# Seven-product FFN stage: transfers in GpSimd's queue, weight sums earlier, two products ahead of the down projection

## The chip, the cores and the metric

One of the eight cores of one Trainium2 chip runs the kernel. The metric is device time in microseconds of one execution, the median of several; lower is better. Everything is float32 in and out.

## The reference

The reference is a two-layer backbone over 512 latent tokens and 256 context tokens (768 rows of 1024), cut here to the parts that the change touches:

```python
mod = silu(c) @ w_mod          # six vectors of 1024 a layer, for latent (c) and context (c_ctx)
h = rms_norm(x, g) * (1 + scale) + shift
x = x + gate1 * (mix(h) @ w_out)             # mixing sub-layer: gMLP, attention, mLSTM
h = rms_norm(x, g) * (1 + scale2) + shift2
x = x + gate2 * swiglu(h)                     # FFN sub-layer

def swiglu(h, w_gate, w_up, w_down):
    return (jax.nn.silu(h @ w_gate) * (h @ w_up)) @ w_down     # D_FF = 2816
```

The context rows go through the same weights. The second layer's modulation needs only the first two of its six vectors for the context.

## The kernel before, in words

Activations lie transposed, 128 features by tokens, latent 512 and context 256 columns. A float32 product is made of three matmuls in the chip's reduced type: every operand is split into a high part (hi, an ACT activation) and the rest (lo, a DVE subtraction), and hi by hi, hi by lo and lo by hi are summed in PSUM. So each weight tile that arrives by DMA (wraw, 128 x 1024, 512 KB) is split into whi and wlo before its matmuls: by `wload` (L130 for the load, L133 and L134 for the split) for ordinary products, by `split_w` (L113, L114) in the seven-product stage. Matmuls into `dps` are ordinary ones (`dense`, L157).

Each engine has its own queue of instructions, in an order that a scheduler fixes when the kernel is built: it walks the instructions as they are written and places them by due times, so the order in the code and the order in the queue differ, but neither changes at run time. Buffers of a pool are shared in turn: an instruction that needs a buffer waits for the last user of what was in it. The pools that matter are `wraw` (4 buffers; loads of w_seven, of w_dn, and of w_mod, named wmod, all use it), whi/wlo of the stage (3), PSUM in `mm` (3) and `mx` (4), and `za`, seven buffers, four of which hold operands during the stage, so that three are left for xs.

Layer 0's FFN is the stage in question, `ffn_seven`. The gate and up products of one pair of 128-wide column blocks are each computed as one 2 x 2 block product by seven half-size products instead of eight, a scheme of Strassen's kind. A **unit** is one of the 22 such products (11 pairs, gate and up). It loads two weight tiles a and b, and forms sums of their quarters on DVE: `sums` makes s1 and s2 and rewrites b, L1243 to L1245; `w4` makes another one, L1255. Its products P1 and P2 (weights of `w1`, tile a), P6 and P5 (`w2`, from s2 and s1), P7 and P4 (`w3`, tile b), and P3 (`w4`) are 12 matmuls of 128 x 384 each, into PSUM banks X, Y and Z. `stage1` is P1 and P2, `stage2` is sums, w2, P6, P5, w3 and P7, `stage3` is w4, P4 and P3. Program order interleaves two units: the stage2 of one, the stage1 of the next, the stage3 of the first. The products of TensorE are pinned in that order. `snap` copies a bank out, and `put` adds, applies Silu or the product of gate and up, and splits the result into gh and gl (L113, L114, L1293).

After the first pair, and then after every two pairs, comes a **down**: the part of w_dn that belongs to the pairs just made is multiplied with gh and gl and added to the residual. The pieces are `FF0_PIECES`: one with nf = 2 (96 matmuls of 512 or 256 columns, in eight steps k), four with nf = 4 (192 matmuls), and a last one that runs into the next layer's norm. One w_dn tile serves two of the eight steps k. The residual x does not fit beside the operands: it lies in DRAM (xd), and for each k a buffer xs is loaded (L1434), the product is added with the gate by `resid` (two DVE steps, L1106), and xs is stored (L1437). All transfers of the stage stand in the queue of SyncE (SPq).

The downs are also where the second layer's modulation vectors are worked out. `mod_steps` yields items, and `feed` takes some of them after each k: an item loads one 128 x 1024 tile of w_mod (L213) and multiplies it with the broadcast condition on DVE, summing along the row (L216), once for each of the two streams (latent and context), or once only for vectors 2 to 5 of layer 1. With two streams the first step's output goes to a second wraw buffer, called junk. Vectors 1 to 5 of layer 1, forty items, are fed in the stage: four in the first down, nine in each of the next four. Vector 0 of layer 1 and vector 5 of layer 0 are fed in layer 0's w_out (sixteen items, thirty-two DVE steps), one or two a k (`fill_rate`).

## Time and profile before

| | us |
|---|---|
| median of 3 runs | 1750.72 (1750.66 to 1758.18) |
| the profiled execution | 1757.62 |
| its span | 1755.6 |
| mean granted TensorE clock | 0.976 |
| layer 0's w_out | about 405 to 477 |
| seven-product stage with its downs | about 477 to 1052 |
| layer 1's mixing and w_out | up to about 1380 |

The page of the profile lists engine busy times, waits by releaser ("PE dps L157 <- ACT whi L133" is the time in which TensorE stood ahead of a matmul into dps and what it waited for last was ScalarE's whi) and groups of instructions by line. PE is TensorE's matmuls and PEld its weight loads, which run ahead of the matmuls and overlap them. DVE is VectorE, ACT ScalarE, POOL GpSimd, SP SyncE, and SPq the DMA issues in SyncE's queue. A row of a table by stretches has the stretch, its length, the busy time and number of instructions of PE, PEld, DVE, ACT and POOL, the granted TensorE clock, the share of time in which the DMA engines were busy, and GB/s. A row of waits has the total, the number and the longest. Matmul ends are modelled.

### The profile page before, as it was taken

To read this page: it belongs to the slowest core of one execution; us is meant where nothing else is said; L and a number is where in the kernel's file an instruction comes from. 1 tells how busy PE (TensorE), PEld (TensorE's weight loads), DVE (VectorE), ACT (ScalarE), POOL (GpSimd) and SP (SyncE) were. 2 spreads that over 40 slices of the span, in tenths; PEclk is the share of its full clock that TensorE was granted. 3 is DMA by queue.
4 is the path that set the end of the run, shared out by engine and by line. 5 is a ranking of instruction groups with operands and counts; after the bars stand their busy time and mean duration, and the time that the engine had idled before them with its cause. 6 is when DMAs were issued, how large, how long until landed. Compare 5 with 4: busy or idle time off the path is not lost.

```text
span 1755.6 us, 26472 instructions
## 1 busy us (share of the span) xinstructions
PE 1632.7 (93%) x10520; PEld 1422.0 (81%) x10520; DVE 1116.1 (64%) x1987; ACT 697.7 (40%) x1277; POOL 167.7 (10%) x157
## 2 busy tenths in 40 slices
PE   7998989988888989989999999989999999999998
PEld 5876777776777969889898988867879988888888
DVE  5598788779786676757567557585585633333335
ACT  5445344642552414234241445534454522222225
POOL 0001122252100000000000030012043100000000
PEclk9998999999998999999999999999999999999999
DMA  8742323245426264562828252211213322222222
GB/s 304 253 154 61 109 77 94 68 134 171 168 75 240 72 227 145 166 206 97 275 73 278 93 178 87 94 57 38 73 61 118 111 96 97 96 96 96 96 79 84
DMA packets 71403, 223.85 MB, mean 128 GB/s; under 512 B 8432, under 2 KB 10096, under 8 KB 71152
## 3 DMA queue, kind: packets, MB, share of 16 engines
q1 hardware_dynamic: 71280, 222.17, 38.3%
q8 instruction: 82, 1.34, 0.3%
q14 instruction: 41, 0.34, 0.1%
HBM read 195.92 MB, written 26.21 MB: 127 GB/s over the span
## 4 chain that ended last, share of the span: by engine, by line
PE 62%; DVE 19%; DMA 8%; ACT 4%; issue 4%; POOL 2%; SPq 0%; DVEq 0%; ACTq 0%; POOLq 0%
PE dps L157 35%; PE X L1264 8%; DMA wmod<-in_w_mod 4%; PE wps L406 4%; PE Z L1264 3%; PE vps L652 3%; PE Y L1264 2%; DMA wraw<-in_w_dn 2%; DVE wlo L134 2%; DVE wmod L216 2%; DVE junk L216 2%; PE bops L546 1%; DMA xd<-xs 1%; PE ptps L588 1%; DVE wlo L114 1%
## 5 line engine op out<-in xcount | busy, mean ns | idle before, releaser
L133 ACT ACTIVATE whi<-wraw 128x1024 fp32r<-128x1024 f32 (+3 forms) x182 | 183.3, 1008 | 471.5 <-PE dps L157 229.5
L134 DVE TENSOR_TENSOR wlo<-wraw,whi 128x1024 fp32r<-128x1024 f32 (+3 forms) x182 | 215.1, 1183 | 140.4 <-ACT whi L133 135.7
L157 PE MATMUL dps<-gh,whi 128*128 128x512 f32 (+1 forms) x576 | 176.7, 348 | 22.2 <-ACT whi L133 15.6
L157 PE MATMUL dps<-gl,whi 128*128 128x512 f32 (+1 forms) x576 | 175.8, 345 | 0.2 <-DVE gl L114 0.2
L157 PE MATMUL dps<-gh,wlo 128*128 128x512 f32 (+1 forms) x576 | 173.8, 344 | 0.2 <-DVE wlo L134 0.2
L157 PE MATMUL dps<-lh,whi 128*128 128x512 f32 x336 | 137.0, 410 | 4.2 <-ACT whi L133 3.4
L157 PE MATMUL dps<-lh,wlo 128*128 128x512 f32 x336 | 136.4, 407 | 2.0 <-DVE wlo L134 2.0
L157 PE MATMUL dps<-ll,whi 128*128 128x512 f32 x336 | 136.8, 408 | 1.5 <-DVE ll L114 1.4
L157 PEld LDWEIGHTS dps<-gh,whi 128*128 128x128 f32 x576 | 100.2, 191 | 39.2 <-ACT whi L133 17.2
L157 PE MATMUL dps<-h2lh,whi 128*128 128x512 f32 (+1 forms) x336 | 128.0, 384 | 0.0
L157 PE MATMUL dps<-h2ll,whi 128*128 128x512 f32 (+1 forms) x336 | 128.0, 384 | 0.0
L157 PE MATMUL dps<-h2lh,wlo 128*128 128x512 f32 (+1 forms) x336 | 127.9, 384 | 0.0
L216 DVE SCALAR_TENSOR_TENSOR wmod<-wmod,c_all 128x1024 f32<-128x1024 f32 x80 | 101.3, 1266 | 22.4 <-DMA wmod<-in_w_mod 21.7
L157 PEld LDWEIGHTS dps<-gl,whi 128*128 128x128 f32 x576 | 100.6, 192 | 14.4 <-DVE gl L114 0.7
L157 PEld LDWEIGHTS dps<-gh,wlo 128*128 128x128 f32 x576 | 99.7, 190 | 13.8 <-DVE wlo L134 0.5
L1106 DVE SCALAR_TENSOR_TENSOR x<-dps,modT,x 128x256 f32<-128x256 f32 (+1 forms) x80 | 46.9, 589 | 94.8 <-PE dps L157 94.2
L114 DVE TENSOR_TENSOR wlo<-wraw,whi 128x1024 fp32r<-128x1024 f32 (+1 forms) x66 | 67.9, 1043 | 35.7 <-ACT whi L113 35.6
L157 PE MATMUL dps<-ch,whi 128*128 128x256 f32 x256 | 76.4, 298 | 14.2 <-DVE bv L525 7.5
L113 ACT ACTIVATE whi<-wraw 128x1024 fp32r<-128x1024 f32 (+1 forms) x66 | 59.4, 913 | 62.7 <-PE Z L1264 19.0
L1264 PE MATMUL X<-ol,whi 128*128 128x384 f32 x242 | 81.8, 338 | 2.6 <-DVE ol L114 2.6
L1264 PE MATMUL X<-oh,whi 128*128 128x384 f32 x242 | 81.7, 338 | 1.3 <-ACT gate L1283 0.9
L1264 PE MATMUL X<-oh,wlo 128*128 128x384 f32 x242 | 81.5, 337 | 1.0 <-DVE wlo L114 1.0
(382 smaller groups left out, 3891.7 us busy)
## 6 DMA issues: line engine op xcount, KB each, us to landing
wmod<-in_w_mod SPq DMA_DIRECT2D x80, 512.0 KB, 3.8
wraw<-in_w_seven SPq DMA_DIRECT2D x44, 512.0 KB, 3.7
wraw<-in_win_blk SPq DMA_DIRECT2D x34, 512.0 KB, 3.6
xs<-xd SPq DMA_DIRECT2D x40, 384.0 KB, 5.0
xd<-xs SPq DMA_DIRECT2D x40, 384.0 KB, 4.4
wraw<-in_w_out SPq DMA_DIRECT2D x23, 512.0 KB, 3.3
wraw<-in_w_dn SPq DMA_DIRECT2D x22, 512.0 KB, 4.1
wraw<-in_w_up SPq DMA_DIRECT2D x21, 512.0 KB, 3.3
```

The lines of the kernel that those rows point to most:

```text
L113: ac.activation(out=hi, in_=src, func=AF.Copy)
L114: ve.tensor_tensor(out=lo, in0=src, in1=hi.bitcast(F32), op=ALU.subtract)
L133: ac.activation(out=hi[:, 0:n], in_=raw[:, 0:n], func=AF.Copy)
L134: ve.tensor_tensor(out=lo[:, 0:n], in0=raw[:, 0:n], in1=hi[:, 0:n].bitcast(F32), op=ALU.subtract)
L157: m = te.matmul(out=ps[:, 0:T], lhsT=wt[:, c], rhs=(flo if wh else fhi)(k), start=(k == 0 and wi == 0), stop=(k == nk - 1 and wi == 2),)
L216: ve.scalar_tensor_tensor(out=wraw.tile([128, D], F32, tag="w", name="junk") if t < nt - 1 else raw, in0=raw, scalar=1.0, in1=c_all[:, t, ...
L406: m = te.matmul(out=ps[:, 0:T], lhsT=wt[:, cs_], rhs=(flo if wh else fhi)(k), start=(k == 0 and wi == 0), stop=(k == KD - 1 and wi == 2))
L546: m = te.matmul(*args, **kw)
L588: te.transpose(out=tps[:, i * 128:(i + 1) * 128], in_=pt[:, i * 128:(i + 1) * 128], identity=ident)
L652: te.matmul(out=vps[i][:, 0:408], lhsT=tokslice(nm, k, i), rhs=wt[:, cs], start=(k == 0 and wi == 0), stop=(k == KD - 1 and wi == 2))
L1106: ve.scalar_tensor_tensor(out=xs, in0=ps, scalar=modT[:, row * 8 + k, g[3]:g[3] + 1], in1=xs, op0=ALU.mult, op1=ALU.add)
L1264: m = te.matmul(out=ps[:, 0:HN], lhsT=wt[:, c], rhs=O[op, j][wh], start=(start and j == 0 and wi == 0), stop=(j == 3 and wi == 2), skip_gr ...
```

## The change

It has five parts.

1. The loads and stores of the residual in the stage (xs, xd, and the first store and the last load of x) and the modulation loads of the stage are issued by GpSimd (`gp`) in place of SyncE (`sp`). SyncE keeps w_seven and w_dn.
2. An item of modulation in the stage is one stream: one load, one DVE step, no junk buffer. Vectors 0 and 1 of layer 1 are so loaded twice, and the stage has 56 items: vectors 0 to 4 of layer 1. They are fed eight in the first down, and twelve in each of the next four.
3. Vector 0 of layer 1 thus leaves layer 0's w_out, which keeps eight items (vector 5 of layer 0, sixteen DVE steps); vector 5 of layer 1 goes to layer 1's w_out, eight items of one step.
4. The next unit's `sums` and `w2` are written ahead of the stage3 of the current unit.
5. P6 and P5 (`stage2a`) of the unit that follows a down are written ahead of the down, and the down's first matmul is pinned behind them.

The queues at the fourth down (w_dn0_3, the one from 826 us in the profile of before). SyncE before, where in_w_dn0_3 is w_dn, wmod a modulation load and the xd and xs rows are residual transfers:

```order
L130 DMA wraw_7687<-in_w_dn0_3 128x1024
L213 DMA wmod_7721<-in_w_mod 128x1024
L213 DMA wmod_7724<-in_w_mod 128x1024
L213 DMA wmod_7759<-in_w_mod 128x1024
L130 DMA wraw_7765<-in_w_dn0_3 128x1024
L213 DMA wmod_7799<-in_w_mod 128x1024
L213 DMA wmod_7833<-in_w_mod 128x1024
L1437 DMA xd_106<-xs_7685 128x768
L130 DMA wraw_7839<-in_w_dn0_3 128x1024
```

GpSimd now, at the same place:

```order
L1452 DMA xs_7778<-xd_106 128x768
L220 DMA wmod_7738<-in_w_mod 128x1024
L220 DMA wmod_7772<-in_w_mod 128x1024
L220 DMA wmod_7775<-in_w_mod 128x1024
L220 DMA wmod_7815<-in_w_mod 128x1024
L1454 DMA xd_106<-xs_7701 128x768
L220 DMA wmod_7849<-in_w_mod 128x1024
L220 DMA wmod_7852<-in_w_mod 128x1024
L1454 DMA xd_106<-xs_7741 128x768
L1452 DMA xs_7818<-xd_106 128x768
```

The modulation loads and the residual's transfers have left SyncE's queue, where they stood between the w_dn loads, and stand together in GpSimd's; in SyncE's the four w_dn loads of this down now follow one another. All of them still take their buffers from the same four of wraw, two of which the next unit's a and b hold during a down. Of the two others, one takes w_dn and modulation loads in turn now (wraw_7703, wmod_7772, wraw_7780, wmod_7849 and so on), the other modulation loads alone.

VectorE ahead of a unit's P6, before. Tiles a and b of this unit are wraw_5654 and wraw_5655; lines L1243 to L1245 are its sums, the two rows into wlo_5735 its splits for P6 and P5, and the first row, from wraw_5517, is the split for P3 of the unit before it; the rows into gate and sn are `put`:

```order
L114 TENSOR_TENSOR wlo_5692<-wraw_5517,whi_5691 128x512
L1289 TENSOR_TENSOR sn_5632<-sn_5632,X_5525 128x384
L1293 TENSOR_TENSOR gate_5497<-gate_5497,sn_5632 128x384
L114 TENSOR_TENSOR gl_5591<-gate_5497,gh_5589 128x384
L1289 TENSOR_TENSOR gate_5726<-sn_5676,Y_5663 128x384
L1243 TENSOR_TENSOR s1_5729<-wraw_5655 128x512
L1244 TENSOR_TENSOR s2_5730<-s1_5729,wraw_5654 128x512
L1245 TENSOR_TENSOR wraw_5655<-wraw_5654,wraw_5655 128x512
L1293 TENSOR_TENSOR gate_5570<-gate_5570,X_5525 128x384
L114 TENSOR_TENSOR wlo_5735<-s2_5730,whi_5734 128x512
L114 TENSOR_TENSOR wlo_5735<-s1_5729,whi_5734 128x512
```

And now, at a unit of the same kind with tiles wraw_5750 and wraw_5751, where wlo_5792 is the split for P6 and P5, and wlo_5799 that for P3 of the unit before it:

```order
L1250 TENSOR_TENSOR s1_5786<-wraw_5751 128x512
L1251 TENSOR_TENSOR s2_5787<-s1_5786,wraw_5750 128x512
L1252 TENSOR_TENSOR wraw_5751<-wraw_5750,wraw_5751 128x512
L114 TENSOR_TENSOR wlo_5792<-s1_5786,whi_5791 128x512
L1296 TENSOR_TENSOR gate_5730<-gate_5730,X_5625 128x384
L114 TENSOR_TENSOR wlo_5792<-s2_5787,whi_5791 128x512
L1262 TENSOR_TENSOR wraw_5750<-wraw_5750,s2_5787 128x512
L1296 TENSOR_TENSOR sn_5772<-sn_5772,Y_5759 128x384
L114 TENSOR_TENSOR wlo_5799<-wraw_5617,whi_5798 128x512
L1300 TENSOR_TENSOR gate_5700<-gate_5700,sn_5772 128x384
```

The three sums and the two splits stood behind the split for P3 of the unit before and four steps of its outputs; they now stand ahead of that split. On TensorE P6 and P5, 24 matmuls into X and Z that stood behind each down's dps rows, stand ahead of them.

The diff (line numbers of the changed kernel are 7 to 18 higher in the stage):

```diff
@@ -114,7 +114,7 @@
         ve.tensor_tensor(out=lo, in0=src, in1=hi.bitcast(F32), op=ALU.subtract)
 
     fill = []
-    last_pe = [None]
+    last_pe, pin_d = [None], [None]
     fill_rate = [FILL_MIX]
 
     chain = [None]
@@ -158,6 +158,9 @@
                         out=ps[:, 0:T], lhsT=wt[:, c], rhs=(flo if wh else fhi)(k),
                         start=(k == 0 and wi == 0), stop=(k == nk - 1 and wi == 2),
                     )
+                    if pin_d[0] is not None:
+                        after(m, pin_d[0])
+                        pin_d[0] = None
                     if i == 1:
                         if share not in (None, True) and k == 0 and wi == 0:
                             after(m, share[1])
@@ -204,19 +207,23 @@
 
     c_all = const.tile([128, 2, D], F32, name="c_all")
 
-    def mod_steps(l, vs):
+    def mod_steps(l, vs, single=False):
         modT, sm = mods[l], smalls[l]
-        items = [(v, i) for v in vs for i in range(KD)]
-
-        def step(v, i):
+        nts = {v: 1 if l == 1 and v >= 2 else 2 for v in vs}
+        if single:
+            items = [(v, i, (t,)) for v in vs for i in range(KD) for t in range(nts[v])]
+        else:
+            items = [(v, i, range(nts[v])) for v in vs for i in range(KD)]
+
+        def step(v, i, ts):
             raw = wraw.tile([128, D], F32, tag="w", name="wmod")
-            sp.dma_start(out=raw, in_=A["w_mod"][l, v, i])
-            nt = 1 if l == 1 and v >= 2 else 2
-            for t in range(nt):
+            (gp if single else sp).dma_start(out=raw, in_=A["w_mod"][l, v, i])
+            nt = nts[v]
+            for t in ts:
                 ve.scalar_tensor_tensor(
-                    out=wraw.tile([128, D], F32, tag="w", name="junk") if t < nt - 1 else raw, in0=raw, scalar=1.0, in1=c_all[:, t, :], op0=ALU.mult, op1=ALU.mult,
+                    out=wraw.tile([128, D], F32, tag="w", name="junk") if t < ts[-1] else raw, in0=raw, scalar=1.0, in1=c_all[:, t, :], op0=ALU.mult, op1=ALU.mult,
                     accum_out=modT[:, v * 8 + i, t:t + 1])
-            if i == KD - 1:
+            if i == KD - 1 and ts[-1] == nt - 1:
                 rows = modT[:, v * 8:v * 8 + 8, 0:nt]
                 ve.tensor_tensor(
                     out=rows, in0=rows, in1=sm["bmod"][:, v * 8:v * 8 + 8].unsqueeze(2).to_broadcast([128, 8, nt]), op=ALU.add)
@@ -226,7 +233,7 @@
                         out=dst[:, :, 0:nt], in0=rows, scalar=1.0, in1=ng.unsqueeze(2).to_broadcast([128, 8, nt]),
                         op0=ALU.add, op1=ALU.mult)
 
-        return [lambda v=v, i=i: step(v, i) for v, i in items]
+        return [lambda a=a: step(*a) for a in items]
 
     def load_small(l):
         t = par.tile([128, NSMALL], F32, tag="small%d" % l, name="small")
@@ -1168,7 +1175,7 @@
                     split(th[:, k, :], tl[:, k, :], hf[k][:, 0:HN])
                     O["B%d1" % (1 + k % 2), k // 2] = (th[:, k, :], tl[:, k, :])
                 else:
-                    sp.dma_start(out=xd[k], in_=x[k][:, 0:768])
+                    gp.dma_start(out=xd[k], in_=x[k][:, 0:768])
             steps2.extend(lambda k=k: step(k) for k in range(KD))
 
         def some_steps(n):
@@ -1319,14 +1326,14 @@
                 self.snap1()
                 self.prod("P2", self.Y)
 
-            def stage2(self):
-                self.sums()
-                self.w2()
+            def stage2a(self):
                 self.prod("P6", self.X, start=False)
                 self.snap2()
                 self.Z = pst(mx, "Z")
                 self.prod("P5", self.Z)
                 self.snap5()
+
+            def stage2b(self):
                 self.w3()
                 self.prod("P7", self.X, start=False)
                 self.fin22()
@@ -1413,35 +1420,45 @@
             units[2].stage1()
             u0.stage3()
             u1.stage3()
+            units[2].sums()
+            units[2].w2()
+            units[2].fin1()
+            units[2].stage2a()
             nu = 2
             for pi in range(len(FF0_PIECES)):
                 nf = FF0_PIECES[pi][1]
                 if pi:
                     for i in range(nf):
                         u = units[nu + i]
-                        u.stage2()
+                        if i:
+                            u.stage2a()
+                        u.stage2b()
                         nxt = units[nu + i + 1] if nu + i + 1 < len(units) else None
                         if nxt is not None:
                             nxt.stage1()
+                            nxt.sums()
+                            nxt.w2()
                         u.stage3()
-                        if nxt is not None and i < nf - 1:
+                        if nxt is not None:
                             nxt.fin1()
+                    if nxt is not None:
+                        nxt.stage2a()
                     nu += nf
                 nf, gpart, dload = down(pi)
+                pin_d[0] = pin[0]
                 if pi < len(FF0_PIECES) - 1:
                     for k in range(KD):
                         xt = zat("xs")
-                        sp.dma_start(out=xt, in_=xd[k])
+                        gp.dma_start(out=xt, in_=xd[k])
                         resid(dense(dload(k), nf, [gpart(g) for g in whole], mm if k % 2 == 0 else mx), k, 5, whole, xt)
-                        feed(1 + (k == 0) if pi else k % 2)
-                        sp.dma_start(out=xd[k], in_=xt)
+                        gp.dma_start(out=xd[k], in_=xt)
+                        feed(1 + k % 2 if pi else 1)
                     pin[0] = last_pe[0]
-                    units[nu].fin1()
                 else:
                     feed(len(fill))
                     x = x_tiles()
                     for k in range(KD):
-                        sp.dma_start(out=x[k][:, 0:768], in_=xd[k])
+                        gp.dma_start(out=x[k][:, 0:768], in_=xd[k])
 
                     def done(g, ssq):
                         norm1_begin(1, h_next, x, groups.index(g), ssq)
@@ -1450,22 +1467,23 @@
                     lagged(dload, nf, gpart, 5, done, *TRAIL[1], eng=gp)
 
         preload(AF.Sqrt, tabled)
-        if not last:
-            fill.extend(mod_steps(0, (5,)) + mod_steps(1, (0,)))
-            fill_rate[0] = 2
+        fill.extend(mod_steps(l, (5,)))
+        fill_rate[0] = 1
         lagged(lambda k: wload(A["w_out"][l, k]), KD,
                lambda g: (lambda k: yv(g, k, 0), lambda k: yv(g, k, 1), g[2]), 2, norm2 if last else norm2_seven,
                *TRAIL[2 * l], between=None if last else lambda: some_steps(2))
         h_next = {}
         if not last:
             feed(len(fill))
-            fill.extend(mod_steps(1, range(1, 6)))
+            fill.extend(mod_steps(1, range(5), True))
             fill_rate[0] = 0
             some_steps(KD if len(steps2) > KD else 0)
             pin[0] = None
             ffn_seven()
             continue
         hp2 = [hpart(h2, g) for g in groups]
+        while fill:
+            fill.pop(0)()
         W_g, W_u = A["w_gate"][l], A["w_up"][l]
         fill_rate[0] = FILL_FF
         for pi, (f0, nf) in enumerate(FF_PIECES):
```

## The prediction

> **What bounds the kernel now.** I read the page first, then the stretches of the seven-product stage cut at the first matmul into dps (the start of a down) and the first one into X behind it, then the waits, and last the DMA queue of SyncE. The page's busy times:
>
> ```profile
> PE 1632.7 (93%) x10520; PEld 1422.0 (81%) x10520; DVE 1116.1 (64%) x1987; ACT 697.7 (40%) x1277; POOL 167.7 (10%) x157
> ```
>
> TensorE is busy 93% of the span, so the change, which leaves every matmul in place, can only win idle time of PE, and only where PE waits. The first five downs, and below them the stretch of four units behind the second (start:end, length, PE busy, PEld, DVE, ACT, POOL, clock, DMA share, GB/s):
>
> ```profile
> 528.00:547.80 19.80, 19.10 (x96) 16.01 (x97) 15.23 (x26) 3.26 (x5) 0.00 (x0) 0.91 0.70 248
> 616.80:660.90 44.10, 35.98 (x194) 30.57 (x193) 31.54 (x55) 5.69 (x7) 0.00 (x0) 0.92 0.74 244
> 723.10:763.80 40.70, 35.60 (x193) 30.59 (x192) 26.93 (x44) 5.82 (x9) 0.00 (x0) 0.96 0.84 272
> 826.00:862.40 36.40, 34.16 (x193) 29.39 (x192) 25.82 (x43) 5.70 (x7) 0.00 (x0) 1.00 0.85 284
> 924.60:962.70 38.10, 35.55 (x193) 30.57 (x193) 26.35 (x44) 5.81 (x8) 0.00 (x0) 0.96 0.83 287
> ...
> 660.90:723.10 62.20, 59.68 (x339) 58.39 (x338) 38.66 (x60) 27.51 (x45) 0.00 (x0) 1.00 0.34 115
> ```
>
> The first row is the short down of the first pair; the four long downs last 44.1, 40.7, 36.4 and 38.1 us, 159.3 together, for 192 matmuls each, which at full clock take 34.2 us of PE. Their DMA share is 0.74 to 0.85, while the units run at 0.34. What PE waits for in the stage from 517 to 1022 (total, times, longest):
>
> ```profile
> PEld dps L157 <- ACT whi L133: 17.2, 5, 7.0
> PE dps L157 <- ACT whi L133: 15.6, 5, 6.6
> PEld X L1264 <- DVE wlo L114: 13.9, 11, 1.3
> PE X L1264 <- DVE wlo L114: 10.1, 11, 1.0
> ...
> PE dps L157 <- ACT gh L113: 6.1, 4, 3.9
> ```
>
> So there are three idle kinds: downs waiting for a split of w_dn, which ScalarE itself waits for from DMA; units waiting for a half-unit's split; and the start of a down waiting for gh.
>
> **The change, part by part.**
>
> Sums half a unit ahead. Before, a unit's three sums and two splits stand in VectorE's queue behind the last output steps of the unit ahead, and its P6 waits for them. In the stretch of four units from 661 to 723:
>
> ```profile
> PEld X L1264 <- DVE wlo L114: 2.6, 2, 1.3
> PE X L1264 <- DVE wlo L114: 2.0, 2, 1.0
> ...
> PEld X L1264 <- ACT whi L113: 1.2, 2, 0.6
> ...
> PE X L1264 <- ACT whi L113: 0.6, 2, 0.3
> ```
>
> That is two places of 1.0 + 0.3 us by the matmuls, or 1.3 + 0.6 by the weight loads ahead of them; I take 1.6 a place. The eleven times of the stage's row, less one at a short down, leave ten: 16 us (13 to 19). They are hidden afterwards by P4 and P3 of the unit before, 24 matmuls of about 0.176 us (59.68 over 339), 4.2 us, against some 2.5 us of DVE work. What is late next is the split for P3, which now waits for a weight buffer that P2 of the next unit frees; its slack is about half a microsecond, so up to 3 of the 16 may stay. **-16.**
>
> P6 and P5 ahead of down. They put 24 matmuls, 4.2 us, where PE waited for gh. In the long downs those waits (6.1 less 3.9 for the first, 2.2) are inside the lengths above. In the short down I give nothing back for the 3.9, for these rows from 547 to 561:
>
> ```profile
> ACT whi L113 <- DVE xs L1106: 4.2, 1, 4.2
> PEld X L1264 <- ACT whi L113: 4.1, 1, 4.1
> DVE xs L1106 <- DMA xs<-xd: 3.8, 2, 3.2
> PE X L1264 <- ACT whi L113: 3.7, 1, 3.7
> ```
>
> P1 of the unit after next waits for a split that queues behind residual steps, and these wait for the load of xs. With P6 and P5 gone from behind the down, P1 comes 4.2 us sooner to the same late residual: what is won ahead is lost there.
>
> Transfers in GpSimd's queue. No transfer of before is issued by GpSimd, so its price has to be bounded. The issues of the down from 826, by SyncE:
>
> ```profile
> 826.71 0.33 SPq L130 DMA_DIRECT2D wraw<-in_w_dn  x1
> 829.94 3.14 SPq L213 DMA_DIRECT2D wmod<-in_w_mod  x2
> ...
> 834.94 0.33 SPq L130 DMA_DIRECT2D wraw<-in_w_dn  x1
> ...
> 847.78 0.43 SPq L130 DMA_DIRECT2D wraw<-in_w_dn  x1
> ```
>
> An issue takes 0.33 us when nothing holds it and 1.57 (half of 3.14) when the queue is held; a cheaper one can save 0.33 at most. I take 0.7, nearer the free one, as nothing computes on GpSimd during a down (POOL 0.00 in the rows above). [...]
>
> The long downs. Each now has twelve modulation loads in place of nine, and the order of the queues has one buffer of the two free ones carry w_dn, modulation, w_dn, modulation in turn. The durations, from the DMA issues of 517 to 963 (KB, median us to landing) and from the groups of 617 to 661 (busy, mean ns):
>
> ```profile
> wmod<-in_w_mod SPq DMA_DIRECT2D x40, 512.0 KB, 3.8
> ...
> xd<-xs SPq DMA_DIRECT2D x39, 384.0 KB, 4.7
> xs<-xd SPq DMA_DIRECT2D x37, 384.0 KB, 5.4
> wraw<-in_w_dn SPq DMA_DIRECT2D x16, 512.0 KB, 4.4
> ```
> ```profile
> L216 DVE SCALAR_TENSOR_TENSOR wmod<-wmod,c_all 128x1024 f32<-128x1024 f32 x9 | 11.0, 1221 | 3.7 <-DMA wmod<-in_w_mod 3.6
> ...
> L134 DVE TENSOR_TENSOR wlo<-wraw,whi 128x1024 fp32r<-128x1024 f32 x3 | 3.7, 1226 | 6.7 <-ACT whi L133 6.7
> ...
> L133 ACT ACTIVATE whi<-wraw 128x1024 fp32r<-128x1024 f32 x3 | 3.2, 1058 | 29.2 <-DMA wraw<-in_w_dn 29.2
> ```
>
> A w_dn load holds its buffer for 4.4 + 1.06 + 1.23 = 6.7 us, a modulation load for 3.8 + 1.22 = 5.0: a round is 11.7, and 12.4 with 0.7 of issue on GpSimd. Counted from the start of the down, I put the second w_dn load at about 2.2 (the modulation load ahead of it in its buffer is out before the down), the third at 14.6, the fourth at 27.0, and its low half at 33.7, say 34.5 behind other DVE steps. Behind that stand a quarter of the down, 34.2 / 4 = 8.5 us, of which the products with the high half can start a microsecond sooner: 42.5 us a down, 170 for the four against 159.3. Before, three loads went out at 0.7, 8.9 and 21.8 us of the 36.4 us down. **+11.** Ends: with the bare round (11.7 and no DVE queueing) the fourth goes out at 25.6 and the down takes about 40, 160 in all, +1; lower, to 38 (-7), only if buffers come free faster than these durations. With 1.57 an issue the round is 13.3, the fourth goes out at 28.8 and the down takes 44.3, +18. The bytes do not forbid 42.5: twelve modulation loads and four of w_dn at 0.52 MB and sixteen of xs at 0.39 are 14.7 MB, against 13.1 with nine, of which the 284 GB/s over 36.4 us moved 10.3 inside the down; with the same 2.8 outside, 11.9 MB over 42.5 us is 280 GB/s.
>
> [...]
>
> The short down. Eight modulation loads in place of four, and three buffers for xs, each of which must be stored (4.7) before it is loaded again (5.4), now in one queue with the modulation loads: two more of these ahead of a load at 1.6 to 2 us each. **+4**, from -4 (the two-buffer steps with junk are gone, and the 3.9 is partly kept) to +8.
>
> Layer 0's w_out, and layer 1's. Here are the stretch and its PE waits from 405 to 477, the groups of its modulation steps, and the stretch ahead of layer 1's w_out:
>
> ```profile
> 405.00:477.00 72.00, 61.35 (x331) 52.64 (x329) 58.04 (x78) 28.43 (x45) 15.29 (x12) 0.93 0.56 188
> 1285.00:1320.00 35.00, 31.69 (x247) 23.93 (x245) 30.08 (x54) 18.76 (x40) 16.05 (x14) 0.95 0.14 46
> ```
> ```profile
> POOL sqacc L257 <- ACT sq L256: 60.3, 12, 14.3
> ...
> PE dps L157 <- ACT whi L133: 6.2, 3, 3.4
> ...
> PE dps L157 <- DVE wlo L134: 4.1, 4, 2.1
> ```
> ```profile
> L216 DVE SCALAR_TENSOR_TENSOR junk<-wmod,c_all 128x1024 f32<-128x1024 f32 x7 | 10.7, 1529 | 0.0
> ...
> L216 DVE SCALAR_TENSOR_TENSOR wmod<-wmod,c_all 128x1024 f32<-128x1024 f32 x7 | 9.7, 1379 | 0.1
> ```
>
> DVE is busy 58 of 72 us there; of 32 modulation steps in and ahead of this stretch 16 go, some 16 x 1.45 = 23 us. Of 10.3 us of waits, the last, near 464 to 469, stands behind the norm's steps and stays, about 4: **-6.3**, from -3 to -9. The eight stores of x, now on GpSimd between its sqacc adds, I cost at nothing: GpSimd waits 60 us for ScalarE's squares in the same stretch, and eight issues fit into that. Eight loads and eight steps of 1.2 us come to layer 1; the order places them mostly in 1285 to 1320, where DVE is busy 30 of 35 us. 10 us of work into 5 us of room: **+4**, from 0 (the rest falls under layer 1's w_out) to +8.
>
> Sum: -16 + 11 + 4 - 6.3 + 4 = -3.3. Against the profiled execution, 1757.62, that is 1754.3; the median of the runs is 1750.72, 6.9 lower, so 1747.4; I write **1747**.
>
> **The rivals.**
>
> Long downs held by the GpSimd queue (slower). A queue issues in order: a modulation load that waits for a buffer holds every store and load of xs behind it, and the DVE step that waits for that xs holds the step which frees the buffer. For it: the waits of before for xs and the 3.14 us of two held issues. Against it: a residual's load stands two or three k ahead. From a round of 14 us on, 1.5 above mine, it decides: the down takes 46, the downs cost +25 and the short one +8, the others as above: +15, 1765. [...]
>
> Bare durations (faster). SyncE's queue now carries w_dn alone, so no load of it waits behind a store. If the round is 11.7 and the added layer 1 steps hide: downs +1, short down 0, units -16, w_out -9, layer 1 0: -24, 1727. For it: DVE is busy 26 of 36 us in the third long down and has room. Against it: the buffers, not the queue, set the round.
>
> The units' waits only move. If P3's split or the gates take over what P6's waited for, the units give -8 in place of -16, the rest as forecast: +5, 1755, no change that can be measured.
>
> **How the numbers follow.** About 0.5%, 8.75 us, is what a measurement can tell from no change, so faster is below 1742 and slower above 1759.5. My own case gets 0.47, with its own range of 1738 to 1757; the slow rival 0.22, the fast one 0.25, the moved waits 0.06. Below 1742 lie the fast rival and a third of my case: 0.41. Above 1759.5 lie the slow rival and some 0.04 of mine: 0.26. The rest is 0.33. The range goes from 1725 to 1768, to both rivals, leaving out 2 in 10.
>
> **What would show it.** Right: no wait of X for wlo or whi at P6; no wait of dps for gh; long downs of 41 to 44 us with the fourth w_dn load some 27 us in; a wait for whi in the last quarter; fewer waits in layer 0's w_out. Wrong: long downs of 36 us or of 46; waits of X at P3; a down that waits for xs; GpSimd issues of over 1.5 us.

## The result and the profile after

The changed kernel takes 1766.8 us (median of five runs, 1765.75 to 1771.83) against 1750.72 before: a ratio of 1.009, interval 1.0063 to 1.0117. Run once more, beside the experiments below, it was 1.005 of the kernel before (1.0031 to 1.0069). It is slower by half a per cent to nearly one, where 0.2% faster was forecast. The profiled execution took 1771.83, its span is 1769.2 (before 1757.62 and 1755.6), and the 13.6 us between the two spans are followed here.

The short down and the four long ones of the changed kernel, and the four units behind the first long one (columns as before: stretch, length, PE, PEld, DVE, ACT, POOL, clock, DMA share, GB/s):

```profile
517.60:550.50 32.90, 21.69 (x97) 18.27 (x96) 18.00 (x30) 3.33 (x5) 10.05 (x19) 0.79 0.74 245
615.40:660.30 44.90, 36.72 (x194) 31.23 (x193) 25.99 (x42) 5.68 (x6) 12.00 (x22) 0.92 0.80 269
719.90:765.80 45.90, 38.16 (x194) 32.58 (x193) 25.66 (x41) 5.67 (x6) 12.00 (x22) 0.89 0.80 264
826.20:872.20 46.00, 38.43 (x193) 32.84 (x193) 24.73 (x40) 5.67 (x6) 12.01 (x22) 0.89 0.81 262
931.70:977.00 45.30, 38.69 (x195) 32.95 (x194) 25.99 (x42) 4.65 (x6) 12.00 (x22) 0.89 0.81 267
660.30:719.90 59.60, 58.89 (x338) 58.45 (x338) 43.79 (x69) 26.73 (x46) 3.27 (x6) 1.00 0.35 115
```

The units are faster: 59.6 us where the same 336 matmuls took 62.2, and PE is busy nearly all of it. The downs are slower. The four long ones take 182.1 us where they took 159.3. Their PE busy time went from 141.3 to 152.0, at a clock of 0.89 to 0.92, so that of the 22.8 us 12.1 are idle and 10.7 are the same matmuls run slower. What PE waits for from 517 to 1030:

```profile
ACT whi L133 <- DMA wraw<-in_w_dn: 148.5, 15, 14.8
PEld dps L157 <- ACT whi L133: 44.2, 10, 8.0
PE dps L157 <- ACT whi L133: 41.0, 10, 7.6
ACT whi L113 <- DMA wraw<-in_w_seven: 33.3, 4, 9.1
...
DVE s L1250 <- DMA wraw<-in_w_seven: 7.1, 5, 2.3
...
PE X L1271 <- DVE wlo L114: 4.7, 4, 1.5
```

The waits of X for wlo, 10.1 us in eleven places before, are down to 4.7 in four, and none for gh is left. The wait for the split of w_dn has gone from 15.6 us in five places to 41.0 in ten. At the fourth down, the w_dn loads in SyncE's queue, and the splits on ScalarE that wait for them:

```profile
827.69 0.33 SPq L130 DMA_DIRECT2D wraw<-in_w_dn  x1
838.71 0.33 SPq L130 DMA_DIRECT2D wraw<-in_w_dn  x1
853.70 0.33 SPq L130 DMA_DIRECT2D wraw<-in_w_dn  x1
```
```profile
830.93 1.06 ACT L133 ACTIVATE whi<-wraw 128x1024 fp32r<-128x1024 f32 x1 [4.05 <-DMA wraw<-in_w_dn]
845.25 1.06 ACT L133 ACTIVATE whi<-wraw 128x1024 fp32r<-128x1024 f32 x1 [13.25 <-DMA wraw<-in_w_dn]
861.07 1.06 ACT L133 ACTIVATE whi<-wraw 128x1024 fp32r<-128x1024 f32 x1 [14.77 <-DMA wraw<-in_w_dn]
```

The loads go out 1.5, 12.5 and 27.5 us after the start of the down; each split starts when its load has landed, so these took at most 3.2, 6.5 and 7.4 us. The last split stands 34.9 us in, and 11.1 us of down follow it. Over the four long downs the last load goes out 26.9, 27.6, 27.5 and 29.1 us in and lands, by the trace, in 6.0, 6.2, 7.3 and 4.9 us, 6.1 on average; before the change the last loads of these downs landed in 5.9, 6.1, 4.9 and 5.3 us. Of the 5.7 us by which a long down is longer on average, 4.0 are that its last load goes out later, 0.5 its landing, and 1.2 what follows its split. Here is the granted clock behind the fourth down's wait:

```profile
862.00:864.00 2.00, 1.83 (x7) 1.59 (x8) 1.85 (x2) 1.07 (x2) 0.87 (x2) 0.68 0.57 202
864.00:866.00 2.00, 2.00 (x8) 1.71 (x7) 1.66 (x3) 0.00 (x0) 0.22 (x1) 0.50 0.81 190
866.00:868.00 2.00, 2.00 (x12) 1.72 (x12) 0.00 (x0) 0.00 (x0) 0.56 (x1) 0.97 0.87 260
```

After a wait of 4.4 us PE runs at half clock for 3.4 us, by these rows: 8 matmuls in 2 us, then 12. So this wait costs some 1.7 us more than its length. The length of a wait alone does not tell here whether the clock falls: in the profile of before a wait of 2.3 us, which ends at 952.7, has 3.4 us at 0.50 behind it, and in the changed kernel one of 2.9 us, which ends at 635.2, has none (1.00 from 635 to 641).

The issues of the stage's transfers, 517 to 990, and three of GpSimd's issues in the fourth down:

```profile
wmod<-in_w_mod POOLq DMA_DIRECT2D x54, 512.0 KB, 4.6
wraw<-in_w_seven SPq DMA_DIRECT2D x36, 512.0 KB, 4.4
xd<-xs POOLq DMA_DIRECT2D x40, 384.0 KB, 5.2
xs<-xd POOLq DMA_DIRECT2D x37, 384.0 KB, 5.2
wraw<-in_w_dn SPq DMA_DIRECT2D x16, 512.0 KB, 4.9
```
```profile
841.26 0.55 POOL L1452 DMA_DIRECT2D xs<-xd  x1 [3.60 <-DMA xd<-xs]
...
847.85 0.55 POOL L220 DMA_DIRECT2D wmod<-in_w_mod  x1 [4.57 <-DVE wlo L134]
...
853.38 0.55 POOL L1452 DMA_DIRECT2D xs<-xd  x1 [2.58 <-DMA xd<-xs]
```

An issue on GpSimd takes 0.55 us. Modulation loads land in 4.6 us (before 3.8), w_dn in 4.9 (4.4), w_seven in 4.4 (3.8). Layer 0's w_out, from 405 to 477, has lost much of its waiting (before 4.1 for wlo and 6.2 for whi), and the stage's first matmul stands at 465.7, where it stood at 477.4:

```profile
PE dps L157 <- DVE wlo L134: 3.5, 1, 3.5
PE dps L157 <- ACT whi L133: 1.2, 1, 1.2
```
```profile
465.67 0.34 PE L1271 MATMUL X<-olh,whi 128*128 128x384 f32 x1
```

Put together, after less before: up to the first X -11.7; the start of the stage, the short down and the units behind it +10.3, of which 4.2 are the two products that now stand ahead of each down; the long downs +22.8; the three stretches of units between them -7.1; the last units -6.0 (4.2 of it those products again); from the last down on +5.3. That is the 13.6.

### The profile page after: what moved, and what is told of

It is laid out like the page before. It is cut to its first block, busy times and chain, and to the rows that moved or that the text cites. A ratio compares the mean times of both kernels' runs of the same rounds, so it can differ in the third digit from the quotient of the medians.

```text
span 1769.2 us, 26551 instructions
## 1 busy us (share of the span) xinstructions
PE 1641.7 (93%) x10520; PEld 1437.6 (81%) x10520; DVE 1121.1 (63%) x1987; ACT 696.3 (39%) x1277; POOL 249.1 (14%) x309
## 4 chain that ended last, share of the span: by engine, by line
PE 56%; DVE 15%; issue 14%; DMA 9%; ACT 3%; POOL 2%; DVEq 0%; SPq 0%; POOLq 0%; ACTq 0%
PE dps L157 35%; DMA wmod<-in_w_mod 5%; PE wps L413 4%; PE X L1271 3%; DMA wraw<-in_w_dn 3%; PE vps L659 3%; DVE wlo L134 2%; PE Z L1271 1%; DVE wmod L223 1%; PE ptps L595 1%; PE bops L553 1%; PE Y L1271 1%; DMA wraw<-in_w_seven 1%; PE bsps L553 1%; DVE wlo L114 1%
## 5 line engine op out<-in xcount | busy, mean ns | idle before, releaser
L157 PE MATMUL dps<-gh,whi 128*128 128x512 f32 (+1 forms) x576 | 182.0, 359 | 41.0 <-ACT whi L133 41.0
L157 PE MATMUL dps<-gl,whi 128*128 128x512 f32 (+1 forms) x576 | 180.0, 355 | 0.0
L157 PE MATMUL dps<-gh,wlo 128*128 128x512 f32 (+1 forms) x576 | 178.2, 352 | 0.3 <-DVE wlo L134 0.3
L223 DVE SCALAR_TENSOR_TENSOR wmod<-wmod,c_all 128x1024 f32<-128x1024 f32 x96 | 122.6, 1280 | 47.5 <-DMA wmod<-in_w_mod 46.8
L157 PEld LDWEIGHTS dps<-gh,whi 128*128 128x128 f32 x576 | 104.2, 200 | 58.3 <-ACT whi L133 44.2
L113 ACT ACTIVATE whi<-wraw 128x1024 fp32r<-128x1024 f32 (+1 forms) x66 | 60.0, 914 | 79.9 <-DMA wraw<-in_w_seven 33.3
L157 PE MATMUL dps<-ch,wlo 128*128 128x256 f32 x256 | 75.6, 295 | 3.5 <-DVE wlo L134 3.5
```

The costliest lines, as they stand in the source:

```text
L113: ac.activation(out=hi, in_=src, func=AF.Copy)
L157: m = te.matmul(out=ps[:, 0:T], lhsT=wt[:, c], rhs=(flo if wh else fhi)(k), start=(k == 0 and wi == 0), stop=(k == nk - 1 and wi == 2),)
L223: ve.scalar_tensor_tensor(out=wraw.tile([128, D], F32, tag="w", name="junk") if t < ts[-1] else raw, in0=raw, scalar=1.0, in1=c_all[:, t, ...
```

## The experiments

The theory after the result: the pace of a down is set by the two weight buffers that w_dn and the modulation loads share, and the change puts more loads through them, so that loads are late and crowd each other. The rival: it is GpSimd's queue. In the tables of lengths "short" is the first down and "long" the four behind it; a version with P6 and P5 ahead of the downs starts them 4.2 us of work later, so its lengths are compared with one another. Ratios are to the kernel before on the same chip. All versions below write the store of xs ahead of `feed`, as the changed kernel does and the kernel before does not; no run parts this from the rest.

**Where the transfers are issued.** All of them back on SyncE, in the changed kernel:

```diff
-            (gp if single else sp).dma_start(out=raw, in_=A["w_mod"][l, v, i])
+            sp.dma_start(out=raw, in_=A["w_mod"][l, v, i])
...
-                        gp.dma_start(out=xt, in_=xd[k])
+                        sp.dma_start(out=xt, in_=xd[k])
...
-                        gp.dma_start(out=xd[k], in_=xt)
+                        sp.dma_start(out=xd[k], in_=xt)
```

(and the stores and loads of x likewise).

> The changed kernel with every transfer of the stage back in SyncE's queue (parts 2 to 5 kept). Buffers theory (the modulation loads that take turns with w_dn in the same two weight buffers, twelve a down, set the round, and transfers in flight together stretch it): the long downs stay at 44 to 47 us and the time at 1762 to 1770. Queue theory (a modulation load held in GpSimd's queue holds the residual's transfers behind it): the long downs fall to 38 to 41, the short one to 20 to 24, and the time to 1730 to 1742.

Measured: 0.9975 (0.9961 to 0.999), 1753.22 us. Short 32.7, long 44.2, 43.5, 43.9, 44.2. Neither theory holds alone. The downs stay long, as the buffers theory has it, and yet the time falls by 0.7 to 1.2% against the changed kernel. The rows of its second down, and of the units behind it:

```profile
602.20:646.40 44.20, 37.13 (x194) 31.72 (x193) 25.80 (x42) 5.67 (x6) 0.00 (x0) 0.92 0.84 285
...
646.40:704.90 58.50, 58.50 (x338) 58.50 (x337) 43.82 (x69) 27.19 (x46) 0.00 (x0) 1.00 0.35 109
```

The down moved 285 GB/s from one queue, where the changed kernel moved 269 from two. The units have no wait left: 58.5 us, PE busy for all of it. In the changed kernel VectorE's sums waited 7.1 us for w_seven in five places, 4.4 to 8.3 us behind the start of each stretch of units; with the transfers on SyncE none of them waits, and PE has no wait for wlo in the units behind the long downs, where it had one of 0.7 to 1.5 us in each stretch. ScalarE's wait for w_seven is not the difference: it is 33.3 us in the one and 30.3 in the other. These rows give the second queue no gain: the down is 0.7 us longer with it (44.9 against 44.2).

The two kinds parted: the first edit of the three alone (modulation loads on SyncE), then the others alone.

> The changed kernel with the modulation loads back on SyncE and the residual's transfers left on GpSimd. If the price of GpSimd's queue is that the two kinds hold each other up in one order, parting them takes nearly all of it away: a ratio to the kernel before of 0.997 to 1.000, as with all of it on SyncE. If each transfer from GpSimd takes longer to land, about half is left: 1.002 to 1.006.

Measured: 1.0 (0.9984 to 1.0016); short 28.4, long 44.8, 42.5, 43.2, 42.8.

> The changed kernel with the residual's transfers back on SyncE and the modulation loads left on GpSimd. Order theory: parted, so 0.997 to 1.000. Landing theory: the modulation loads gate w_dn, so more than half is left: 1.003 to 1.008.

Measured: 1.0072 (1.0053 to 1.0091); short 32.2, long 47.1, 47.6, 47.1, 47.5. So the residual's traffic on GpSimd costs little (1.0 against 0.9975), and the modulation loads on GpSimd nearly all of it (1.0072), although they had the queue for themselves. The first of the two runs alone would have fitted the idea that the two kinds hold each other up in one queue; by the second it falls. That was the rival of the prediction in its own words.

**How many loads.** The modulation fed as before, the transfers still on GpSimd:

```diff
-        fill.extend(mod_steps(l, (5,)))
-        fill_rate[0] = 1
+        if not last:
+            fill.extend(mod_steps(0, (5,)) + mod_steps(1, (0,)))
+            fill_rate[0] = 2
...
-            fill.extend(mod_steps(1, range(5), True))
+            fill.extend(mod_steps(1, range(1, 6)))
...
-                        feed(1 + k % 2 if pi else 1)
+                        feed(1 + (k == 0) if pi else k % 2)
```

(with the issue of these loads on GpSimd kept for layer 1's).

> The changed kernel with the modulation fed as before (two streams an item, vectors 1 to 5 in the stage, four items in the short down and nine in each long one, vector 0 in layer 0's w_out), the transfers still in GpSimd's queue. Buffers theory: the long downs fall to 37 to 41 us and the short one to 20 to 24, while layer 0's w_out gets its 12 us back: 1740 to 1750. Queue theory: the long downs stay above 43 and the time rises to 1770 to 1780, since w_out's gain is gone.

Measured: 0.9942 (0.9926 to 0.9958), 1747.75 us. Short 28.8, long 48.2, 39.4, 37.4, 38.1. Three of the four long downs came back; the first, where the last two-stream items are fed, each with a second buffer, did not. The same with the transfers on SyncE, which leaves parts 4 and 5 of the change alone:

> The kernel before with the sums half a unit ahead and P6 and P5 ahead of the down alone: all transfers in SyncE's queue, the modulation fed as before. Both theories: units without their P6 waits (13 to 16 us less), downs as before or a little shorter at their start: 1732 to 1740. If a weight buffer that the earlier sums hold longer takes it back, 1748 or more.

Measured: 0.9858 (0.9839 to 0.9876), 1732.81 us. Short 28.6, long 40.6, 37.5, 38.6, 35.9. Two parts of the five are worth 24 us; the other three take more than that away. By the ratios GpSimd's queue (part 1) costs 0.8% with the modulation fed as before (0.9858 to 0.9942), and parts 2 and 3 cost 1.2% with all transfers on SyncE (0.9858 to 0.9975), although they win time in w_out. Part 4 alone, with P6 and P5 left behind the down:

```diff
-            units[2].fin1()
-            units[2].stage2a()
...
-                        if i:
-                            u.stage2a()
+                        u.stage2a()
...
-                    if nxt is not None:
-                        nxt.stage2a()
```

> The kernel before with the sums and their splits half a unit ahead alone; P6 and P5 stay behind the down. If the units' P6 waits are what part 4 is worth, 0.990 to 0.992 of the kernel before (14 to 17 us), and parts 4 and 5 together (0.986) leave 7 to 10 us to the two products ahead of the down. If the earlier sums are what shortens the downs too, 0.987 or less.

Measured: 0.9976 (0.9958 to 0.9994), 1753.01 us. Less than was expected of it. The units behind the second down, the second and the third down, and the stage's waits at the downs:

```profile
616.80:665.20 48.40, 37.88 (x194) 32.29 (x194) 30.37 (x51) 4.83 (x6) 0.00 (x0) 0.86 0.72 235
723.70:762.60 38.90, 34.88 (x194) 29.46 (x193) 25.66 (x42) 4.80 (x6) 0.00 (x0) 1.00 0.88 298
...
665.20:723.70 58.50, 58.50 (x338) 58.50 (x337) 40.58 (x62) 27.88 (x47) 0.00 (x0) 1.00 0.32 102
```
```profile
PE dps L157 <- ACT whi L133: 32.7, 13, 9.4
```

The units gave all that was forecast, 3.7 us a stretch of four, but the downs took it back: the waits for the split of w_dn went from 15.6 to 32.7 us. Its w_dn loads go out 5.1 us after the start of the third to fifth down, not 0.5 to 1.7 as before. The loads are not later in themselves: counted from the end of the down before they go out after 63.6 us, where they went out after 62.7 to 63.9 us. It is the down that starts 3.7 us sooner, and its loads do not. With P6 and P5 ahead of it, in the version with parts 4 and 5, the same loads go out 0.9 to 1.0 us into the down. So the two products ahead of the down are worth not just the waits for gh that they cover, but some 20 us on top of the sums by the ratios (0.9976 to 0.9858); of the 15.9 us between the two profiled executions 7.8 lie in the first long down and 6.9 in the three others.

**What crowds.** The changed kernel without the residual's traffic (it leaves out the residual's sum of five downs):

```diff
-                        gp.dma_start(out=xt, in_=xd[k])
+                        gp.memset(xt[:, 0:768], 0.5)
...
-                        gp.dma_start(out=xd[k], in_=xt)
+                        gp.dma_start(out=xd[k][:, 0:96], in_=xt[:, 0:96])
```

> The changed kernel without the residual's traffic in the first five downs: a memset on GpSimd in place of each load of xs, and a store of 96 of its 768 columns (the residual's sum is so left out). If transfers in flight together stretch the landing of w_dn (6.5 to 7.3 us for the third and fourth load of a down in the changed kernel against 3.2 for the second, which is alone), they land in 3.2 to 4.5 us and the long downs take 40 to 42 us. If the count of loads through the two buffers sets the pace alone, the landings stay and the downs stay at 45 to 46.

Measured: 1725.28 us in one run, so there is no interval and the reading rests on the rows of this one profile. The short down 26.3, the long ones 38.9, 38.3, 37.4, 38.7, below what either theory gave. The fourth down, and its w_dn loads and splits:

```profile
799.60:837.00 37.40, 34.42 (x194) 29.32 (x193) 25.73 (x41) 4.62 (x5) 12.94 (x22) 1.00 0.64 207
```
```profile
801.22 0.33 SPq L130 DMA_DIRECT2D wraw<-in_w_dn  x1
812.49 0.33 SPq L130 DMA_DIRECT2D wraw<-in_w_dn  x1
823.89 0.33 SPq L130 DMA_DIRECT2D wraw<-in_w_dn  x1
```
```profile
815.74 1.06 ACT L133 ACTIVATE whi<-wraw 128x1024 fp32r<-128x1024 f32 x1 [9.99 <-DMA wraw<-in_w_dn]
827.42 1.06 ACT L133 ACTIVATE whi<-wraw 128x1024 fp32r<-128x1024 f32 x1 [10.62 <-DMA wraw<-in_w_dn]
```

With the same loads through the same buffers the w_dn loads go out 1.6, 12.9 and 24.3 us in, a round of 11.4 (the 11.7 of bare durations, within 0.3), and the last two land in 3.2 and 3.5 us, not 6.5 and 7.4. The clock is 1.00. The residual's traffic, then, is worth 7.2 us a long down on average: 2.8 because the last load goes out sooner (25.0 us in, not 27.8), 2.5 in its landing (3.6 against 6.1), and 1.9 behind its split, where PE runs at half clock less (the clock of the long downs is 0.96 to 1.00, not 0.89 to 0.92). That the landings stretch with this traffic is shown. What the run takes away is more than bytes in flight, though: also the residual's place in GpSimd's queue and the steps' waits for xs. The first is not what counts, since the long downs stay at 47 us with the residual's transfers in SyncE's queue (1.0072 above); the second is 4.4 us in the whole stage of the changed kernel.

**Versions meant to be better.** If the loads through the two buffers are the trouble, one load should serve both streams, and the first stream's product, which is thrown away, should not take a weight buffer. It is written in half width to one of the small buffers; forty items remain in the stage:

```diff
-    out=wraw.tile([128, D], F32, tag="w", name="junk") if t < ts[-1] else raw, ...
+    out=wk.tile([128, D], mybir.dt.bfloat16, tag="wk", name="junk") if t < ts[-1] else raw, ...
...
-            fill.extend(mod_steps(1, range(5), True))
+            fill.extend(mod_steps(1, range(5)))
...
-                        feed(1 + k % 2 if pi else 1)
+                        feed(1 + (k == 0) if pi else k % 2)
```

All transfers are on SyncE, parts 3 to 5 kept.

> A version meant to beat both: parts 2 to 5 with all transfers on SyncE, but one load for both streams of a modulation item, whose first product goes to a small half-width buffer in place of a weight buffer (it is thrown away); forty items in the stage, as before, vector 0 out of layer 0's w_out. Buffers theory: the loads through the two buffers fall from 56 to 40, so the downs go back to 36 to 39 us while w_out keeps its 12 us: a ratio of 0.978 to 0.982 (1715 to 1725). If VectorE's steps set the pace, the downs stay at 42 to 44: 0.995.

Measured: 1.0062 (1.0038 to 1.0087). A miss, and not of the stage: its long downs take 40.6, 39.9, 35.3 and 34.7. The stage's first matmul stands at 500.7, 35 us later than in the changed kernel:

```profile
500.74 0.34 PE L1271 MATMUL X<-olh,whi 128*128 128x384 f32 x1
```

Layer 0's modulation, ahead of the stage, used the small buffers too. So the edit was confined to layer 1 (`if l` in the choice of the buffer):

> As one_load, but the small buffer for the product that is thrown away is used in the stage alone (layer 1's vectors); layer 0's modulation, which the earlier version slowed ahead of the stage, is as before. One load for both streams, forty items, all transfers on SyncE, parts 3 to 5. Buffers theory: against all_sp (56 loads) the long downs fall from 44 to 35 to 40 us and nothing else moves: 0.980 to 0.985 of the kernel before. If the count of loads isn't the pace, 0.997 as all_sp.

Measured: 0.9843 (0.982 to 0.9865), 1730.12 us. Short 26.5, long 42.6, 42.1, 35.7, 37.5. As the buffers theory has it: against all transfers on SyncE with 56 loads (0.9975), 40 loads take 1.3% off. The number of DVE steps in the stage is 56 in both, but not their places: the first long down now has eighteen in place of twelve, the last two nine. That the steps set the pace is the rival, and the first long down speaks against it, with six steps more and three loads fewer it takes 42.6 us and not 44.2. The two downs with two-stream items, where a load holds its buffer for two DVE steps, gain least. Then without modulation in the short down, `feed(1 + (k in (0, 4)) if pi else 0)`:

> The same, with no modulation in the short down and ten items in each long one. If the short down's fourth w_dn load waits for modulation loads alone, the short down falls from 29 to 21 us and each long one rises by 1 to 2: within 3 us of one_load_stage, either way. If the residual's three buffers hold the short down, it stays above 26 and the time rises by 4 to 8.

Measured: 0.985 (0.9829 to 0.9871). Short 18.5, long 45.5, 46.0, 40.7, 40.1: the short down's wait was modulation alone, and a tenth item costs a long down 3 to 5 us (in the second one some of it may be two-stream items that have moved there).

> The changed kernel once more, on the same chip as the two versions above: 1.007 to 1.011 of the kernel before, long downs of 45 to 46 us.

Measured: 1.005 (1.0031 to 1.0069), a little under what was expected; long 42.6, 44.3, 45.7, 45.1.

And with nine items in each long down and four left over for the last, `feed(1 + (k == 0) if pi else 0)`:

> one_load_stage with no modulation in the short down and nine items in each long one; the four items left over are fed ahead of the last down. If modulation loads between w_dn loads are all that holds the short down and the tenth item is what made the long ones 3 to 5 us longer in one_load_late, the short down takes 18 to 19 us, the long ones 35 to 43 as in one_load_stage, and the time is 5 to 8 us below it: 0.979 to 0.982 of the kernel before. If the last down has no room for four loads, they cost what was won: 0.984.

Measured: 0.9775 (0.9754 to 0.9796), 1718.52 us, the best of all. Its downs:

```profile
519.10:537.30 18.20, 17.05 (x98) 14.52 (x97) 12.74 (x20) 3.77 (x5) 0.00 (x0) 1.00 0.79 267
596.30:636.70 40.40, 36.18 (x194) 30.58 (x194) 31.55 (x50) 4.62 (x5) 0.00 (x0) 0.96 0.75 261
696.70:737.50 40.80, 36.39 (x194) 30.65 (x193) 30.76 (x50) 4.62 (x5) 0.00 (x0) 0.96 0.77 261
796.20:832.00 35.80, 34.07 (x193) 29.24 (x192) 21.88 (x35) 4.62 (x5) 0.00 (x0) 1.00 0.86 282
892.40:928.10 35.70, 34.05 (x193) 29.36 (x193) 21.76 (x35) 4.62 (x5) 0.00 (x0) 1.00 0.84 289
```

The short down and the last two long ones are within 2 us of PE's own time, at full clock.

**GpSimd's queue by itself.** Both runs move one kind of transfer to GpSimd in this best version, as in the diffs above.

> one_load_end (0.9775 of the kernel before) with the modulation loads of the stage issued by GpSimd. If a load from GpSimd goes out and lands later by itself, some 0.5 us each, four gating loads a long down and the w_seven loads behind them cost 6 to 12 us: 0.981 to 0.985. If the price comes only with crowded buffers: 0.976 to 0.979.

Measured: 0.9879 (0.9858 to 0.9901), 1734.74 us; short 18.2, long 44.6, 45.7, 36.8, 40.0.

> one_load_end with the residual's transfers issued by GpSimd, so that SyncE's queue holds no wait for a store. If a queue of their own frees the weights' loads, 0.973 to 0.976. If the stores and loads of xs from GpSimd only land later (5.2 us against 3.8 and 4.5), 0.978 to 0.981.

Measured: 0.9832 (0.9811 to 0.9853), 1726.46 us; short 22.6, long 40.8, 43.3, 36.5, 38.8. GpSimd's queue costs in a kernel without too many loads as well, 18 us for the modulation and 10 for the residual, more than was expected. How it does so isn't settled. A modulation load goes out 0.3 us after the step that frees its buffer, where SyncE's goes out within 0.05; its issue takes 0.2 longer, and it lands in 4.4 us against 4.0. But moving a transfer to another queue also changes the order that the scheduler makes and with it which buffer a load gets, so the runs don't part the queue from the order. No issue on GpSimd is seen to be held: in the changed kernel every one but the first, 0.72 us, took 0.54 to 0.56, and with the modulation loads alone in that queue 0.53. Why the loads land later is open.

## Why the prediction was wrong

It forecast 1747, 0.2% faster, with a chance of 0.26 for slower by over 0.5%; it is slower. 1766.8 lies at the very end of the range. That the slow rival gave 1765 is luck: it needed a round of 14 us by modulation loads that hold the residual's transfers behind them in GpSimd's queue. That queue does cost, but not by this hold, and over half of what the long downs miss the forecast by comes from landings.

By place in the profiled executions, after less before, with the two products that moved ahead of each down counted where they stood:

| | forecast, us | measured, us |
|---|---|---|
| up to the first X (layer 0's w_out) | -6.3 | -11.7 |
| start of the stage, short down, units behind it | +4 - 3.2 | +6.1 |
| four long downs | +11 | +22.8 |
| three stretches of units between them | -9.6 | -7.1 |
| last units | -3.2 | -1.8 |
| from the last down on (layer 1) | +4 | +5.3 |
| sum | -3.3 | +13.6 |

Of the 16.9 us of miss 11.8 are the long downs. The misses at w_out and at the short down, over 5 us each, cancel, which is luck too. By the terms of the sum:

- **The long downs, +11.** This is the step that failed, in size and most of all in the landing of the last w_dn load: +22.8, or 3.0 us a down more than the 42.5 that were forecast. The last load goes out at 27.8 us on average where 27.0 was put (+0.8), it lands in 6.1 us and not 4.4 (+1.7), and 11.6 us of down follow the start of its split, not 11.1 (+0.5). The 4.4 was the median of all w_dn loads; the one that is waited for goes out with the residual's and the modulation's transfers in flight (at the fourth down a load of xs goes out 0.3 us ahead of it and a store 1.3 us behind, and the DMA engines are busy 0.84 of its 7.4 us), and before the change too it landed in 4.9 to 6.1 us. Without the residual's traffic it landed in 3.6 and the downs took 38.3. With all transfers on SyncE the four downs take 175.8 us in place of 182.1, so some 6 of the 12 us go with GpSimd's queue. The issue time came out right in part by luck: at the fourth down the two rounds were 11.0 and 15.0 us, not 12.4 twice. The slow clock, 10.7 of the 22.8 us by PE's busy time, was no term of its own; behind the last split it took up what had been set aside for the low half and the DVE queue. The bytes were counted and found to fit, but the mean rate, 262 to 269 GB/s in these downs, did not tell the 6.1 us of the load that is waited for.
- **Units, -16.** Right in mechanism, too large for the changed kernel. The stretches of four went from 62.2 to between 59.5 and 60.4, 7.1 us for three, and the last units gave 1.8, where eight places of 1.6 make 12.8. The rest is taken back in the first unit behind each down, where the sums wait for a late w_seven load. With the transfers on SyncE the stretches take 58.5, the whole of the term and a little more.
- **P6 and P5, nothing beside the gh waits.** Wrong as a mechanism: they let the down start 4.2 us later against its w_dn loads. Part 4 without part 5 gave 0.2%, both 1.4%. What they are worth in the changed kernel no run shows.
- **The short down, +4.** Too small. The 1.6 to 2 us for a load ahead in the queue was the author's estimate; by two of the versions the four loads of the short down cost it 8.0 us (26.5 with them, 18.5 without), 2.0 each. If the two places at P6 in the units behind it gave their 3.2 us, the term is about +9, just over the top of its range. Eight modulation loads stood between four w_dn loads; with none and all transfers on SyncE the short down takes 18 us.
- **Layer 0's w_out, -6.3.** Right for the waits: over the last 360 matmuls ahead of the first X PE's idle time fell from 11.8 to 5.7 us. Another 3.4 us are the same matmuls run faster (mean clock 0.93 before, 0.95 after), and 2.3 lie ahead of these; neither was in the sum.
- **Layer 1, +4.** Right: between the matmuls that stood at 1283 and 1320 us before, the changed kernel falls back by 4.0 us. The other 1.3 lie elsewhere behind the last units.
- **An issue on GpSimd, 0.7.** The issue takes 0.55 us, but the queue costs 13 to 20 us in all (all transfers on SyncE against the changed kernel, by the ratios). From the first X to the end of the last down it is 593.0 us against 575.1: 11 of these 18 us lie in the units and 6 in the long downs. The prediction gave the move no gain and no loss but that issue. Its upper bound, 1.57 us for an issue that is held, was a misreading: the row of 3.14 us is two issues of 0.33 and the time between them, so it shows no held issue, neither for the top of the range nor for the slow rival:

```profile
829.94 0.33 SPq L213 DMA_DIRECT2D wmod<-in_w_mod  x1
...
832.75 0.33 SPq L213 DMA_DIRECT2D wmod<-in_w_mod  x1
```

## What to carry to other kernels

A load that shares buffers with what it must not wait for was gated here by the other's whole life in the buffer (rounds of 11.0 and 15.0 us at the fourth down), and moving the other to a second queue did not change that (long downs of 43.5 to 44.2 us from one queue, 44.9 to 46.0 from two): count the loads through a buffer, and how long each holds it, before and after. Price the wait that ends last with the landing of that same load, from the time of most traffic, not with the median of all (6.1 us here against 4.4), and look in the granted clock for what follows a wait: here half clock for 3.4 us behind one of 4.4. An edit that makes one stage faster brings the next stage nearer to its loads, which may not come sooner (here a down started 3.7 us sooner and its loads did not). Two edits that depend on each other are worth testing apart and together: parts 4 and 5 gave 0.2% and 1.4%, and with three more the kernel was slower than before.

## What the hardware showed that was not expected

The same transfers moved at 276 to 291 GB/s in the long downs from SyncE's queue alone (parts 2 to 5) and at 262 to 269 when most came from GpSimd's (the changed kernel). Why is open. And at the fourth down of the changed kernel a landing of w_dn took 3.2 us with the DMA engines busy 0.58 of that time, 6.5 at 0.97 and 7.4 at 0.84: the longest is not where their share is highest.
